# A mixture-of-experts block on one core: each expert's down part queued behind the next expert's gate and up part

## The chip, the core and the metric

The kernel runs on one core of one Trainium2 chip. The metric is the device time in microseconds of one execution; the time of a kernel is the median of its runs. The engines are named as in the profile: PE is TensorE (matmul), PEld its weight load, DVE is VectorE, ACT is ScalarE, POOL is GpSimd, SP is SyncE, from whose queue the loads are issued.

## The reference

One block over 256 tokens of width 1024: a mixer (sparse attention, a state-space branch and memory attention, gated and merged), a layer norm, a mixture of 32 experts with 4 experts for each token, and a last layer norm. The change touches the experts and the last norm:

```python
h = _layer_norm(DEEPNORM_ALPHA * h + mix, ln1_g[l], ln1_b[l])
...
logits = (xt @ w_router + b_router).astype(F32)
top_val, top_idx = lax.top_k(logits, TOP_K)          # TOP_K = 4 of 32
gate = jax.nn.softmax(top_val, axis=-1)
...
def expert_block(args):
    xb, e = args
    gu = xb @ w_gate_up[e] + b_gate_up[e]            # 1024 x 2048
    g, lin = jnp.split(gu, 2, axis=-1)
    g = jnp.minimum(g, SWIGLU_LIMIT)
    lin = jnp.clip(lin, -SWIGLU_LIMIT, SWIGLU_LIMIT)
    act = g * jax.nn.sigmoid(SWIGLU_ALPHA * g) * (lin + 1.0)
    return act @ w_down[e] + b_down[e]               # 1024 x 1024
...
out = jnp.zeros((T + 1, D), ys.dtype).at[slot_tok].add(ys)[:T]   # weighted by gate
...
h = _layer_norm(DEEPNORM_ALPHA * h + ffn, ln2_g[l], ln2_b[l])
```

All of it is float32. The weights of the experts alone are 32 x 12 MiB.

## The kernel before, in words

The program is written with tiles; a scheduler orders the instructions of each engine by a simulated run of the program and draws an instruction ahead of an earlier one where it is ready sooner. Each engine then works through its own list in order.

**The front** (lines 175 to 980) is the mixer, the first norm and the router. It keeps its data in slots of 8 KB a partition: tags u, w, s and z with 11, 3, 4 and 4 slots (L47). The weights of the experts go into the same slots. `chunk` (L73) loads one chunk of 1 MiB from SP's queue (L76). `load_chunk(e, c)` (L155) loads chunk c of expert e: chunks 0 to 7 are rows of `w_gate_up`, 8 to 11 of `w_down`; the tag comes from PATTERN (L48) by a running index over all chunks, so the slots are used in turn. `load_some` (L169) loads the first five chunks while the front still works.

**The experts** (L1006 to L1116). `expert` is called 32 times in a Python loop. Each call handles up to 64 tokens of its expert (CAP). Its parts, in program order:

- Gather (L1009 to L1029): `oh` marks the token of each of the 64 places. 48 bf16 matmuls (three bf16 parts of the activations, two token tiles, eight feature tiles) pick the tokens into two PSUM tiles, `xg0` and `xg1`, of four feature tiles each. DVE multiplies each half by the norm's gain, POOL adds the norm's offset: `xT`.
- `pw` (L1034): two transposes of the gate weights, read by DVE into `ohT` and `gs`. `pw` and `pt` are two buffers of the tag "pt".
- Gate and up (L1042 to L1054): bias matmuls, then for each of 8 chunks four matmul pairs into PSUM `pg` and `pl`; the two column halves go to partitions 0 to 63 and 64 to 127. A chunk's slot is free when both `pg` and `pl` matmuls have read it.
- `last()` (L1055), the combination of the expert before: eight matmuls (L1098) scatter its scaled result `ys` to the tokens, DVE adds them to `acc` (L1100).
- SwiGLU in two halves of 256 columns on DVE and ACT (L1064 to L1073), with four transposes into `pt`, copied by ACT into `aT`.
- Down (L1077 to L1084): two PSUM tiles `py`, in the banks of the tags "pg" and "pl"; a bias matmul each, then 32 matmuls over 4 chunks.
- Eviction (L1088 to L1090): ACT scales `py` by `gs`, DVE forms the remainder: `ys`, one buffer for each half.

At expert 0 `then` adds the residual, at expert 1 it counts whether an expert has more than 64 tokens; the loop for such experts (L1130 to L1157) has no turns with these inputs. At expert 31 the last norm's vectors are spread (L1109 to L1112).

**The last norm** (L1119 to L1178). `statistics` over four quarters, the mean and variance, then on three quarters ACT subtracts the mean and POOL multiplies by the gain, on the fourth DVE does both (L1168 to L1176), while DVE forms the inverse root (`inv_sqrt`, L103: 12 instructions on two values each). Then DVE scales and adds on each quarter (L1177) and the quarter is stored, token tile 0 from SP's queue, token tile 1 from ACT's (L1178).

Of the kernel before, what the change touches and what calls it, by code (L numbers as in the profile page):

```python
# [23 lines left out]
NT = 2  # L24
KT = 8
# [33 lines left out]
def block_kernel(ctx: ExitStack, tc: tile.TileContext, a: dict, out: bass.AP):  # L59
# [19 lines left out]
    def tt(o, x, y, op):  # L79
        V.tensor_tensor(o, x, y, op=op)  # L80
# [925 lines left out]
    def expert(mp, pm, gu, dn, pick_e, pos_e, gate_e, slots, then=None, last=None):  # L1006


        sel = mp.tile([128, CAP], BF, tag="sel", name="sel")  # L1009
# [8 lines left out]
        for i in range(2):  # L1018
            ks = slice(4 * i, 4 * i + 4)
            xg = pm.tile([128, 4, CAP], F32, tag=f"xg{i}", name="xg", bufs=1)  # L1020
            for k in range(4):
                n = 0
                for b in range(3):
                    for t in range(NT):
                        PE.matmul(xg[:, k, :], hb[t][b][:, (4 * i + k) * 128:(4 * i + k + 1) * 128], oh[:, t, :],  # L1025
                                  start=n == 0, stop=n == 5)
                        n += 1
            tt(xT[:, ks], xg, lc[:, 0, ks, None].to_broadcast([128, 4, CAP]), OP.mult)
            gg(xT[:, ks], xT[:, ks], lc[:, 1, ks, None].to_broadcast([128, 4, CAP]), OP.add)  # L1029
# [7 lines left out]
        ohT = mp.tile([128, 256], F32R, tag="ohT", name="ohT")  # L1037
        gs = mp.tile([128, 1], F32, tag="gs", name="gs")
# [6 lines left out]
        def up(p_, o, lhsT, w, start, stop):  # L1045
            for hf in range(2):
                PE.matmul(p_[hf * 64:(hf + 1) * 64, :], lhsT, w[:, o + hf * 512:o + (hf + 1) * 512],  # L1047
                          start=start, stop=stop)
# [11 lines left out]
        pt = pm.tile([128, 512], F32, tag="pt", name="pt", bufs=2)  # L1060
        aT = mp.tile([128, 512], F32, tag="aT", name="aT", bufs=1)
        halves = [slice(i * 256, (i + 1) * 256) for i in range(2)]
        g2 = gc.rearrange("p (q c i) -> p q c i", q=2, i=2)
        for sl in halves:  # L1064
            V.tensor_scalar(gc[:, sl], pg[:, sl], LIMIT, None, op0=OP.min)  # L1065
            S.activation(sg[:, sl], gc[:, sl], AF.Sigmoid, scale=SWIGLU_ALPHA)  # L1066
            tt(gc[:, sl], gc[:, sl], sg[:, sl], OP.mult)
        for i, sl in enumerate(halves):
            V.tensor_scalar(lin[:, sl], pl[:, sl], LIMIT, -LIMIT, op0=OP.min, op1=OP.max)
            V.scalar_tensor_tensor(gc[:, sl], lin[:, sl], 1.0, gc[:, sl], op0=OP.add, op1=OP.mult)  # L1070
            for c in (2 * i, 2 * i + 1):
                PE.transpose(pt[:, c * 128:(c + 1) * 128], g2[:, i, :, c % 2], ident)  # L1072
            S.activation(aT[:, sl], pt[:, sl], AF.Copy)  # L1073
        a4 = aT.rearrange("p (c h s) -> p h c s", c=4, h=2)


        pys = [pm.tile([128, 512], F32, tag=tag, name="py", bufs=1) for tag in ("pg", "pl")]  # L1077
        for hf, py in enumerate(pys):
            PE.matmul(py[0:64, :], sel, bias[:, 2 * DFF + hf * 512:2 * DFF + (hf + 1) * 512], start=True, stop=False)  # L1079
        for k in range(0, KT, 2):  # L1080
            for hf, py in enumerate(pys):
                for j in range(2):
                    PE.matmul(py[j * 64:(j + 1) * 64, :], a4[:, k // 4, k % 4 + j, :], dn(k + j, hf),  # L1083
                              start=k + j == 1, stop=k == 6)  # L1084
        ys = []
        for hf, py in enumerate(pys):

            y2 = mp.tile([128, 2, 512], F32R, tag=f"ys{hf}", name="ys", bufs=1)  # L1088
            S.activation(y2[:, 0], py, AF.Copy, scale=gs)  # L1089
            V.scalar_tensor_tensor(y2[:, 1], py, gs, y2[:, 0].bitcast(F32), op0=OP.mult, op1=OP.subtract)  # L1090
            ys.append(y2)

        def combine():
            for hf in range(2):
                for t in range(NT):
                    pc = pm.tile([128, 512], F32, tag="pc", name="pc", bufs=2)
                    for i in range(2):
                        PE.matmul(pc, ohT[:, t * 128:(t + 1) * 128], ys[hf][:, i], start=i == 0, stop=i == 1)  # L1098
                    o = acc[:, t, hf * 512:(hf + 1) * 512]
                    tt(o, o, pc, OP.add)  # L1100
        return combine

    gb2 = vectors(a["ln2_g"], a["ln2_b"])
    last = None
# [166 lines left out]
```

## Time and profile before

| What | Value |
|---|---|
| Median of 3 runs | 1286.26 us (1285.35 to 1784.17) |
| The profiled execution's own time | 1288.12 us |
| Its span, first to last instruction | 1286.4 us |
| Mean granted TensorE clock | 0.983 |
| PE busy | 1216.3 us, 95% of the span |
| PEld busy | 607.8 us, 47% |
| DVE busy | 585.9 us, 46% |
| ACT busy | 294.0 us, 23% |
| POOL busy | 72.6 us, 6% |
| DMA | 451.98 MB, mean 351 GB/s |

Times in the views count from the first instruction of the span. The matmuls' ends are modelled, so a busy PE is not PE at its peak. A wait is put down to what came last before it ended. A chunk is one DMA issue of 1024 KB. The experts' matmuls begin at 348 us and end at 1270 us.

### The profile page before, as it was taken

The page shows a single profiled execution, that of the slowest core. Times are in us where ns is not written, and L with a number is a line of the kernel's source. Part 1 is how long each engine was busy: PE and PEld are TensorE (multiplying, and loading weights), DVE is VectorE, ACT ScalarE, POOL GpSimd, SP SyncE. Part 2 cuts the span into 40 slices and gives each one's busy share as a digit, 9 for nine tenths or more (in the row PEclk, how much of TensorE's full clock was granted, in tenths as well). Part 3 has the DMA queues.
Part 4 walks back from the last instruction along what each step waited for, and adds up shares of the span by engine and source line. Part 5 has one row for each costly group of instructions (what it writes and reads, how often), then busy time and mean ns, then how long its engine had stood idle before and what let it go on. Part 6 is the DMA issues. An engine that isn't in the chain of part 4 may idle for free. (4 is left out here: it accounts for less than half of the span.)

```text
span 1286.4 us, 18050 instructions
## 1 busy us (share of the span) xinstructions
PE 1216.3 (95%) x7277; PEld 607.8 (47%) x7278; DVE 585.9 (46%) x1326; ACT 294.0 (23%) x580; POOL 72.6 (6%) x139
## 2 busy tenths in 40 slices
PE   7999999999799999999999999999999999999994
PEld 6657888788544443333333333333334333333331
DVE  6599986657832432333334333333334333333225
ACT  4245569963210110100001101000011011000011
POOL 1000000000200000000000000000001000000001
PEclk9999999999799999999999999999999999999997
DMA  7335535447799999999999999999999999999991
GB/s 271 108 129 192 195 133 153 158 167 314 265 406 422 426 426 427 426 426 426 427 426 426 427 425 427 426 426 426 427 425 427 426 426 426 426 427 426 426 415 66
DMA packets 65335, 451.98 MB, mean 351 GB/s; under 512 B 8896, under 2 KB 9056, under 8 KB 11360
## 3 DMA queue, kind: packets, MB, share of 16 engines
q1 hardware_dynamic: 64960, 450.26, 85.1%
q8 instruction: 59, 0.97, 0.3%
q10 hardware_dynamic: 288, 0.52, 0.1%
q14 instruction: 28, 0.23, 0.0%
HBM read 449.70 MB, written 1.05 MB: 350 GB/s over the span
## 5 line engine op out<-in xcount | busy, mean ns | idle before, releaser
L1047 PE MATMUL pg<-w,xT 128*64 128x512 f32 x1024 | 266.0, 597 | 0.0
L1047 PE MATMUL pl<-w,xT 128*64 128x512 f32 x1024 | 262.7, 592 | 0.0
L1083 PE MATMUL py<-w,aT 128*64 128x512 f32 x1024 | 230.2, 602 | 0.0
L1065 DVE TENSOR_SCALAR gc<-pg 128x256 f32<-128x256 f32 x64 | 24.2, 420 | 336.3 <-PE pg L1047 336.3
L1090 DVE SCALAR_TENSOR_TENSOR ys<-py,gs,ys 128x512 fp32r<-128x512 f32 x64 | 48.0, 751 | 210.9 <-ACT ys L1089 207.5
L1047 PEld LDWEIGHTS pl<-w,xT 128*64 128x64 f32 x1024 | 78.8, 137 | 133.6 <-issue 125.7
L1083 PEld LDWEIGHTS py<-w,aT 128*64 128x64 f32 x1024 | 71.3, 138 | 133.8 <-issue 127.8
L1047 PEld LDWEIGHTS pg<-w,xT 128*64 128x64 f32 x1024 | 71.9, 136 | 129.6 <-issue 116.0
L1066 ACT ACTIVATE sg<-gc 128x256 f32<-128x256 f32 x64 | 23.1, 408 | 477.0 <-DVE gc L1065 477.0
L80 DVE TENSOR_TENSOR h<-h,pc 128x512 f32<-128x512 f32 x128 | 82.6, 684 | 57.0 <-PE pc L1098 55.3
L83 POOL TENSOR_TENSOR xT<-xT,lc 128x256 f32<-128x256 f32 x64 | 44.9, 702 | 784.7 <-PE py L1079 778.4
L1089 ACT ACTIVATE ys<-py,gs 128x512 fp32r<-128x512 f32 x64 | 44.0, 687 | 195.1 <-PE py L1083 195.1
L1098 PE MATMUL pc<-ys,ohT 128*128 128x512 f32 x256 | 85.5, 435 | 0.9 <-DVE h L80 0.8
L1098 PEld LDWEIGHTS pc<-ys,ohT 128*128 128x128 f32 x256 | 40.2, 188 | 65.8 <-issue 35.1
L187 DVE TENSOR_TENSOR hl<-w,hl 128x1024 fp32r<-128x1024 f32 x48 | 58.2, 1222 | 18.1 <-ACT hl L186 17.8
L201 PE MATMUL mm<-hTh,hl 128*128 128x256 f32 x192 | 56.0, 292 | 0.1
L199 PE MATMUL mm<-hTh,hl 128*128 128x256 f32 x192 | 55.8, 291 | 0.0
L200 PE MATMUL mm<-hTl,hl 128*128 128x256 f32 x192 | 55.4, 289 | 0.0
L186 ACT ACTIVATE hl<-w 128x1024 fp32r<-128x1024 f32 x48 | 49.8, 1053 | 17.8 <-PE mm L201 9.6
L1073 ACT ACTIVATE aT<-pt 128x256 f32<-128x256 f32 x64 | 24.5, 383 | 120.8 <-PE pt L1072 117.4
L1025 PE MATMUL xg<-oh,hb 128*128 128x64 bf16 x1280 | 51.3, 195 | 0.9 <-DVE oh L1015 0.9
L1025 PEld LDWEIGHTS <-hb 128*128 128x128 bf16 x1280 | 47.5, 99 | 9.3 <-issue 8.2
(399 smaller groups left out, 1518.9 us busy)
## 6 DMA issues: line engine op xcount, KB each, us to landing
w<-in_w_gate_up SPq DMA_DIRECT2D x256, 1024.0 KB, 19.6
w<-in_w_down SPq DMA_DIRECT2D x128, 1024.0 KB, 19.6
w<-in_w_g SPq DMA_DIRECT2D x12, 1024.0 KB, 4.9
w<-in_w_s_glu SPq DMA_DIRECT2D x4, 1024.0 KB, 5.5
w<-in_w_o SPq DMA_DIRECT2D x4, 1024.0 KB, 5.8
w<-in_w_memk SPq DMA_DIRECT2D x2, 1024.0 KB, 10.5
w<-in_w_u SPq DMA_DIRECT2D x2, 1024.0 KB, 8.6
w<-in_w_memv SPq DMA_DIRECT2D x2, 1024.0 KB, 5.1
```

What stands on the lines that cost most here:

```text
L80: V.tensor_tensor(o, x, y, op=op)
L83: G.tensor_tensor(o, x, y, op=op)
L186: S.activation(hi, src, AF.Copy)
L187: (eng or V).tensor_tensor(lo, src, hi.bitcast(F32), op=OP.subtract)
L199: PE.matmul(o, lhsT(0), rhs(0), start=start, stop=False)
L200: PE.matmul(o, lhsT(0), rhs(1), start=False, stop=False)
L201: PE.matmul(o, lhsT(1), rhs(0), start=False, stop=stop)
L1025: PE.matmul(xg[:, k, :], hb[t][b][:, (4 * i + k) * 128:(4 * i + k + 1) * 128], oh[:, t, :], start=n == 0, stop=n == 5)
L1047: PE.matmul(p_[hf * 64:(hf + 1) * 64, :], lhsT, w[:, o + hf * 512:o + (hf + 1) * 512], start=start, stop=stop)
L1083: PE.matmul(py[j * 64:(j + 1) * 64, :], a4[:, k // 4, k % 4 + j, :], dn(k + j, hf), start=k + j == 1, stop=k == 6)
L1090: V.scalar_tensor_tensor(y2[:, 1], py, gs, y2[:, 0].bitcast(F32), op0=OP.mult, op1=OP.subtract)
L1098: PE.matmul(pc, ohT[:, t * 128:(t + 1) * 128], ys[hf][:, i], start=i == 0, stop=i == 1)
```

## The change

The load order: after the eight gate and up chunks of expert e come the four down chunks of expert e-1. `expert` no longer runs its down part; it returns two functions, `transposes` and `down`. The loop calls expert e, then the down part of expert e-1, then the transposes of expert e (`issue_after` puts what stands in its block behind the named instruction on that engine); the bias matmuls of gate and up follow the transposes of the expert before. The combination of expert e-2 stands in expert e's gate and up part, one half of the columns after chunk 3 and one after chunk 5. At the end the combination of expert 30, the down part of expert 31 and its combination follow. PSUM: `xg` is one tile of one bank, evacuated whole by one DVE and one POOL instruction; `pw` and `pt` share one buffer; `py0` and `py1` have banks of their own. `sel`, `ohT` and `gs` have three buffers. SwiGLU runs over 512 columns at a time. The last norm: DVE alone subtracts, multiplies and scales, after the inverse root, by token tiles; a token tile's first quarter is stored from SP's queue, the second from ACT's.

```diff
@@ load_some
+    order = [(0, c) for c in range(KT)]
+    for e in range(1, 4):
+        order += [(e, c) for c in range(KT)] + [(e - 1, c) for c in range(KT, 12)]
...
-            early.append(load_chunk(len(early) // 12, len(early) % 12))
+            early.append(load_chunk(*order[len(early)]))
@@ expert
-        for i in range(2):
-            ks = slice(4 * i, 4 * i + 4)
-            xg = pm.tile([128, 4, CAP], F32, tag=f"xg{i}", name="xg", bufs=1)
...
-            tt(xT[:, ks], xg, lc[:, 0, ks, None].to_broadcast([128, 4, CAP]), OP.mult)
-            gg(xT[:, ks], xT[:, ks], lc[:, 1, ks, None].to_broadcast([128, 4, CAP]), OP.add)
+        xg = pm.tile([128, KT, CAP], F32, tag="xg", name="xg", bufs=1)
...
+        tt(xT, xg, lc[:, 0, :, None].to_broadcast([128, KT, CAP]), OP.mult)
+        gg(xT, xT, lc[:, 1, :, None].to_broadcast([128, KT, CAP]), OP.add)
...
-        pw = pm.tile([128, 512], F32, tag="pt", name="pw", bufs=2)
+        pw = pm.tile([128, 512], F32, tag="pt", name="pw", bufs=1)
...
-        up(pg, 0, sel, bias, True, False)
-        up(pl, DFF, sel, bias, True, False)
+        with tc.issue_after(after.ins) if after else ExitStack():
+            up(pg, 0, sel, bias, True, False)
+            up(pl, DFF, sel, bias, True, False)
         for k in range(KT):
             w = gu(k)
             up(pg, 0, xT[:, k, :], w, False, k == KT - 1)
-            up(pl, DFF, xT[:, k, :], w, False, k == KT - 1)
-        if last:
-            last()
+            end = up(pl, DFF, xT[:, k, :], w, False, k == KT - 1)
+            if last and k in (3, 5):
+                with tc.issue_after(end.ins):
+                    last(k // 5)
...
+        V.tensor_scalar(gc, pg, LIMIT, None, op0=OP.min)
+        S.activation(sg, gc, AF.Sigmoid, scale=SWIGLU_ALPHA)
+        V.tensor_scalar(lin, pl, LIMIT, -LIMIT, op0=OP.min, op1=OP.max)
+        tt(gc, gc, sg, OP.mult)
+        V.scalar_tensor_tensor(gc, lin, 1.0, gc, op0=OP.add, op1=OP.mult)
+        def transposes():
+            pt = pm.tile([128, 512], F32, tag="pt", name="pt", bufs=1)
+            aT = mp.tile([128, 512], F32, tag="aT", name="aT", bufs=1)
+            for c in range(4):
+                end = PE.transpose(pt[:, c * 128:(c + 1) * 128], g2[:, c // 2, :, c % 2], ident)
+            S.activation(aT, pt, AF.Copy)
+            ats.append(aT.rearrange("p (c h s) -> p h c s", c=4, h=2))
+            return end
+        def down():
+            a4 = ats[0]
+            pys = [pm.tile([128, 512], F32, tag=f"py{i}", name="py", bufs=1) for i in range(2)]
...
+            def combine(*hfs):
+                for hf in hfs:
...
+            return combine, end
+        return transposes, down
@@ the loop over experts
+        weights(e, 0, KT)
+        if e:
+            weights(e - 1, KT, 12)
         if e == NE - 1:
+            weights(e, KT, 12)
...
+        last = None
+        if before:
+            last, end = before[1]()
+            with tc.issue_after(end.ins):
+                after = part[0]()
+        else:
+            after = part[0]()
+        before = part
+    if last:
+        last(0, 1)
+    before[1]()[0](0, 1)
@@ the last norm
-    quarters = [(t, i, acc[:, t, i * 512:(i + 1) * 512]) for i in range(2) for t in range(NT)]
-    nmu = fin.tile([128, NT], F32)
-    V.tensor_scalar(nmu, mv[:, :, 0], -1.0, None, op0=OP.mult)
-    for t, i, o in quarters[:3]:
-        S.activation(o, o, AF.Identity, bias=nmu[:, t:t + 1])
-        gg(o, o, l2[:, 0, i], OP.mult)
+    quarters = [(t, i, acc[:, t, i * 512:(i + 1) * 512]) for t in range(NT) for i in range(2)]
...
     for t, i, o in quarters:
-        if (t, i) == (1, 1):
-            V.scalar_tensor_tensor(o, o, nmu[:, t:t + 1], l2[:, 0, i], op0=OP.add, op1=OP.mult)
+        V.scalar_tensor_tensor(o, o, mv[:, t, 0:1], l2[:, 0, i], op0=OP.subtract, op1=OP.mult)
         V.scalar_tensor_tensor(o, o, rs[:, t:t + 1], l2[:, 1, i], op0=OP.mult, op1=OP.add)
-        (S if t else nc.sync).dma_start(out[t * 128:(t + 1) * 128, i * 512:(i + 1) * 512], o)
+        (S if i else nc.sync).dma_start(out[t * 128:(t + 1) * 128, i * 512:(i + 1) * 512], o)
```

## Rows read from the trace of the kernel before

**Rows 1.** Busy time by stretches of the span (the columns: the stretch and its length in us, then busy us and instruction count of PE, PEld, DVE, ACT and POOL, the granted clock of TensorE as a share of full speed, the mean busy share of the DMA engines, and GB/s): the last stretch before the experts' steady stage, an early one, and one of the steady stage.

```profile
340.00:360.00 20.00, 17.16 (x136) 8.17 (x137) 14.04 (x45) 0.00 (x0) 3.25 (x6) 0.81 0.66 248
...
380.00:400.00 20.00, 19.50 (x132) 9.81 (x130) 7.41 (x20) 1.49 (x4) 1.59 (x3) 1.00 0.98 397
...
600.00:700.00 100.00, 96.47 (x554) 36.80 (x552) 33.82 (x72) 9.96 (x20) 5.21 (x9) 1.00 1.01 426
```

**Rows 2.** Whom the DMA queue of SyncE waited for after 500 us (waiter, what ended the wait: total us, times, longest us). L76 issues the weight loads.

```profile
SPq L76 <- DMA w<-in_w_gate_up: 410.5, 200, 3.4
SPq L76 <- DMA w<-in_w_down: 205.2, 99, 3.4
...
SPq L76 <- PE pl L1047: 8.7, 21, 2.9
SPq L76 <- PE py L1083: 6.6, 13, 1.9
```

**Rows 3.** Whom TensorE waited for between 500 and 1215 us, all rows of the answer (same columns).

```profile
PE py L1079 <- DVE lin L1069: 19.0, 24, 0.8
PE pt L1072 <- ACT aT L1073: 8.2, 25, 0.6
PE pt L1072 <- DVE gc L1070: 2.0, 2, 1.3
```

**Rows 4.** Timeline of TensorE over one expert of the steady stage (start us, us taken, engine, line, operation, tiles, count; in brackets the idle time just before it). Lines of the pages: L1047 gate and up, L1079 bias of the down part, L1083 down part, L1098 combination.

```profile
1019.86 1.03 PE L1047 MATMUL pl<-w,xT 128*64 128x512 f32 x4
...
1022.08 0.40 PE L1079 MATMUL py<-bias,sel 128*64 128x512 bf16 x1 [0.79 <-DVE lin L1069]
...
1025.29 7.09 PE L1083 MATMUL py<-w,aT 128*64 128x512 f32 x32
1032.37 0.73 PE L1098 MATMUL pc<-ys,ohT 128*128 128x512 f32 x2
...
1033.49 0.74 PE L1098 MATMUL pc<-ys,ohT 128*128 128x512 f32 x2
...
1036.24 1.20 PE L1098 MATMUL pc<-ys,ohT 128*128 128x512 f32 x4
...
1054.02 7.09 PE L1083 MATMUL py<-w,aT 128*64 128x512 f32 x32
```

**Rows 5.** Timeline of SyncE's queue: the issues of the last expert's weights (start us, us from the first to the end of the last issue, count).

```profile
1212.78 17.60 SPq L76 DMA_DIRECT2D w<-in_w_gate_up  x8
1232.48 7.65 SPq L76 DMA_DIRECT2D w<-in_w_down  x4
```

**Rows 6.** DMA issues by line, whole span: the loads of w_down (count, KB each, median us from issue to landing).

```profile
w<-in_w_down SPq DMA_DIRECT2D x128, 1024.0 KB, 19.6
```

**Rows 7.** Busy time by stretches of 1 us at the end of the transfers (columns as in group 1).

```profile
1258.00:1259.00 1.00, 0.82 (x4) 0.51 (x6) 0.00 (x0) 0.40 (x2) 0.00 (x0) 0.90 0.29 123
1259.00:1260.00 1.00, 1.00 (x4) 0.24 (x2) 0.00 (x0) 0.10 (x1) 0.00 (x0) 0.50 0.08 33
1260.00:1261.00 1.00, 1.00 (x4) 0.24 (x2) 0.00 (x0) 0.00 (x0) 0.00 (x0) 0.50 0.00 0
1261.00:1262.00 1.00, 1.00 (x6) 0.32 (x4) 0.00 (x0) 0.00 (x0) 0.00 (x0) 0.50 0.00 0
```

**Rows 8.** Timeline of all engines over the last expert and the final norm (columns as in group 4).

```profile
1239.83 1.08 PE L1047 MATMUL pg<-w,xT 128*64 128x512 f32 x4
...
1254.25 1.03 PE L1047 MATMUL pl<-w,xT 128*64 128x512 f32 x4
...
1258.61 8.78 PE L1083 MATMUL py<-w,aT 128*64 128x512 f32 x32
...
1266.64 0.69 ACT L1089 ACTIVATE ys<-py,gs 128x512 fp32r<-128x512 f32 x1 [7.54 <-PE py L1083]
...
1274.33 0.17 DVE L1167 TENSOR_SCALAR nmu<-mv 128x2 f32<-128x2 f32 x1
...
1275.33 3.70 POOL L83 TENSOR_TENSOR h<-h,l 128x512 f32<-128x512 f32 x3 [78.78 <-ACT h L1169]
1275.40 1.22 DVE L109 TENSOR_SCALAR nr_y<-nr_w 128x2 int32<-128x2 int32 x1
...
1279.09 0.16 DVE L117 SCALAR_TENSOR_TENSOR nr_y<-nr_w,nr_y 128x2 f32<-128x2 f32 x1
```

**Rows 9.** Groups of instructions between 600 and 1200 us, shapes kept apart: the two that evacuate the gather (busy us, mean ns of one, then idle time before and its releaser).

```profile
L83 POOL TENSOR_TENSOR xT<-xT,lc 128x256 f32<-128x256 f32 x42 | 29.5, 702 | 566.9 <-PE py L1079 566.9
...
L80 DVE TENSOR_TENSOR xT<-xg,lc 128x256 f32<-128x256 f32 x42 | 15.7, 416 | 0.0
```

**Rows 10.** Timeline of TensorE over the first two experts: first gate matmul, first part of expert 0's down part, first gate and first up-bias matmul of expert 1.

```profile
348.18 1.08 PE L1047 MATMUL pg<-w,xT 128*64 128x512 f32 x4
...
366.41 1.94 PE L1083 MATMUL py<-w,aT 128*64 128x512 f32 x8
...
376.29 5.74 PE L1047 MATMUL pg<-w,xT 128*64 128x512 f32 x25
381.45 0.38 PE L1047 MATMUL pl<-bias,sel 128*64 128x512 bf16 x1
```

**Rows 11.** Busy time by stretches of 5 us, just before the first expert's matmuls (columns as in group 1).

```profile
345.00:350.00 5.00, 5.00 (x78) 3.75 (x77) 3.57 (x14) 0.00 (x0) 1.22 (x2) 0.76 0.02 7
```

**Rows 12.** Timeline of all engines at the very end: the last products of the norm.

```profile
1280.55 2.74 DVE L1177 SCALAR_TENSOR_TENSOR h<-h,nr_y,l 128x512 f32<-128x512 f32 x4
```

More of the change, by code (lines that the diff above doesn't have):

```diff
@@ L1004, in block_kernel, with expert @@
     pm = main.enter_context(tc.tile_pool(name="pm", bufs=1, space=PSUM))
-    def expert(mp, pm, gu, dn, pick_e, pos_e, gate_e, slots, then=None, last=None):
-        sel = mp.tile([128, CAP], BF, tag="sel", name="sel")
+    def expert(mp, pm, gu, dn, pick_e, pos_e, gate_e, slots, then=None, last=None, after=None):
+        sel = mp.tile([128, CAP], BF, tag="sel", name="sel", bufs=3)
         G.tensor_copy(sel, pick_e.to_broadcast([128, CAP]))
@@ L1068, in expert @@
[L1068 to L1077, printed above, removed]
@@ L1093, in combine @@
[L1093 to L1101, printed above, removed]
-    gb2 = vectors(a["ln2_g"], a["ln2_b"])
-    last = None
+        V.tensor_scalar(gc, pg, LIMIT, None, op0=OP.min)
@@ new lines, in down @@
+        def down():
+            a4 = ats[0]
+            pys = [pm.tile([128, 512], F32, tag=f"py{i}", name="py", bufs=1) for i in range(2)]
+            for hf, py in enumerate(pys):
+                PE.matmul(py[0:64, :], sel, bias[:, 2 * DFF + hf * 512:2 * DFF + (hf + 1) * 512],
+                          start=True, stop=False)
+            for k in range(0, KT, 2):
+                for hf, py in enumerate(pys):
+                    for j in range(2):
+                        end = PE.matmul(py[j * 64:(j + 1) * 64, :], a4[:, k // 4, k % 4 + j, :], dn(k + j, hf),
+                                        start=k + j == 1, stop=k == 6)
+            ys = []
+            for hf, py in enumerate(pys):
+                y2 = mp.tile([128, 2, 512], F32R, tag=f"ys{hf}", name="ys", bufs=1)
+                S.activation(y2[:, 0], py, AF.Copy, scale=gs)
+                V.scalar_tensor_tensor(y2[:, 1], py, gs, y2[:, 0].bitcast(F32), op0=OP.mult, op1=OP.subtract)
+                ys.append(y2)
+            def combine(*hfs):
+                for hf in hfs:
+                    for t in range(NT):
+                        pc = pm.tile([128, 512], F32, tag="pc", name="pc", bufs=2)
+                        for i in range(2):
+                            PE.matmul(pc, ohT[:, t * 128:(t + 1) * 128], ys[hf][:, i], start=i == 0, stop=i == 1)
+                        o = acc[:, t, hf * 512:(hf + 1) * 512]
+                        tt(o, o, pc, OP.add)
+            return combine, end
@@ L1105, in block_kernel, with weights @@
+        return transposes, down
+    gb2 = vectors(a["ln2_g"], a["ln2_b"])
+    last = before = after = None
+    ws = {}
+    def weights(e, lo, hi):
+        for c in range(lo, hi):
+            ws[e, c] = chunks.pop(0) if chunks else load_chunk(e, c)
+    chunks = list(early)
     for e in range(NE):
-        cs = [early[c + 12 * e] if c + 12 * e < len(early) else load_chunk(e, c) for c in range(12)]
-        gw, dw = cs[:KT], cs[KT:]
+        weights(e, 0, KT)
+        if e:
+            weights(e - 1, KT, 12)
@@ L1112, in block_kernel @@
                     [128, 512], F32, tag="pc", name="pc", bufs=2)), AF.Copy)
-        last = expert(mp, pm, lambda k: gw[k], lambda k, c: dw[k // 2][:, k % 2 * 1024 + c * 512:k % 2 * 1024 + (c + 1) * 512],
-               stack[:, e:e + 1], lambda t: posm[:, t, e:e + 1], lambda t: gmat[:, t, e:e + 1], slot,
-               residual if e == 0 else further_blocks if e == 1 else None, last)
-    last()
+        part = expert(mp, pm, lambda k, e=e: ws[e, k],
+                      lambda k, c, e=e: ws[e, KT + k // 2][:, k % 2 * 1024 + c * 512:k % 2 * 1024 + (c + 1) * 512],
+                      stack[:, e:e + 1], lambda t: posm[:, t, e:e + 1], lambda t: gmat[:, t, e:e + 1], slot,
+                      residual if e == 0 else further_blocks if e == 1 else None, last, after)
+        last = None
[9 more added lines that the diff above has]
+    before[1]()[0](0, 1)
     main.close()
@@ L1154, in dn @@
                     return dws[k // 2][:, k % 2 * 1024 + c * 512:k % 2 * 1024 + (c + 1) * 512]
-                expert(op, opm, gu, dn, pick_e, lambda t: pos_e[:, t:t + 1], lambda t: gate_e[:, t:t + 1], slot)()
+                part = expert(op, opm, gu, dn, pick_e, lambda t: pos_e[:, t:t + 1], lambda t: gate_e[:, t:t + 1],
+                              slot)
+                part[0]()
+                part[1]()[0](0, 1)
         statistics()
```

41 lines of the change are left out of this document (12 added, 29 removed).

## The prediction

> **What bounds the kernel now.** First the stretches [rows 1]: which stage owns the time. In the stage of the experts the transfers run at a share of 1.01 and 426 GB/s while TensorE is 96% busy, so two engines look full at once. An expert is 12 chunks of 1 MiB, 12.58 MB: 29.5 us at that rate, 2.46 us a chunk. Second, what the DMA queue waits for [rows 2]: after 500 us it waits 615.7 us for earlier weight loads and 15.3 us for the two PE lines that give slots back. Slots are not short there; transfers pace transfers. Third, TensorE's own waits [rows 3]: 29.2 us over 25 experts, 1.17 us an expert, all on DVE or ACT around the SwiGLU, none on a transfer. TensorE never runs out of weights; it is behind them. One expert's timeline gives the pace [rows 4]: one down part starts at 1025.29 and the next at 1054.02, a period of 28.73 us, 0.77 us under the transfers' 29.5. So TensorE pays off, at 0.77 us an expert, a backlog that it had from the start.
>
> How much is left at the end? The last expert's gate and up chunks are issued in 17.60 us from 1212.78, its last down chunk at about 1239.8 [rows 5], and a chunk lands 19.6 us after its issue [rows 6]: the first of them at 1232.4, the very last at 1259.4. The windows agree: 33 GB/s between 1259 and 1260, then nothing [rows 7]. I take 1260.0 for the last landing and its signal. TensorE starts that expert at 1239.83, 7.4 us behind its first chunk, ends gate and up at 1255.28, starts down at 1258.61 and ends it at 1267.39 [rows 8]. The transfers would allow an end near 1262. After 1267.39 comes one serial chain (eviction, combination, statistics, norm, store), 20.7 us to the execution's 1288.12 us. So the transfers are the floor, and the change can win only what lies behind their end, and what they lose before 400 us.
>
> **The change part by part.**
>
> *The down part one expert later, with the load order.* Between gate and up (end 1020.89) and down (1025.29) TensorE now spends 4.40 us on the next gather, on transposes and on waits [rows 4]. With the previous expert's down part there, 7.08 us long, the SwiGLU has cover, and the 1.17 us of waits go: 28.73 - 1.17 = 27.56 us. No DMA is added or dropped: 12 issues an expert on SyncE's queue, slots dealt by the same running index, and the new order of loading is the new order of use, so no slot is held longer in the queue. Hence the transfers keep their 29.5 us and nothing of the 1.17 us an expert shows directly: it pays off the backlog. 7.4 us over 30 experts needs 0.25 us, so any period up to 28.48 us makes TensorE wait for transfers at the end. What is late next is the last chunk. Backwards from 1260.0: expert 30's last down chunk now lands four chunks earlier, 1250.2; its matmuls take a quarter of 7.09 us, 1.77 us: 1252.0. Next on TensorE stand four transposes, beside the eviction of expert 30 (0.69 us on ACT [rows 8] and, as an estimate, as much on DVE: about 1.5 us), then the combination of expert 30, eight matmuls, 0.73 + 0.74 + 1.20 = 2.67 us [rows 4]: 1256.2. The down part of expert 31 takes 7.09 us, its last chunk being there when its turn comes at 1261.5: end 1263.3. Gain 1267.4 - 1263.3 = 4.1 us. Bounds: 5.6 us (1261.8, if nothing stands before the last chunk) and 0 (the backlog stays).
>
> *PSUM regrouped: the gather.* It is now evacuated whole. A half costs 0.42 us on DVE and 0.70 us on GpSimd [rows 9], so the whole 2.24 us before the first gate matmul may start. In the steady stage it costs nothing as long as the gather is drawn a whole down part ahead, as it is today (before 1025.29, used after 1032.37); without that cover it costs up to 2.24 us an expert, about 1 us of it beside bias matmuls and transposes. For expert 0 there is no cover: the first gate matmul, at 348.18 [rows 10], needed one half and now needs both, 1.12 us more (bounds 0 and 2.24). The transfers stand still just then, 7 GB/s from 345 to 350 [rows 11], until that expert gives slots back, so this passes to all that follows: -1.1 us.
>
> *PSUM regrouped: own banks for the down part.* Today expert 1's gate part runs 25 matmuls from 376.29 before the first one of its up part, at 381.45, whose bank the down part still holds [rows 10]. A chunk is free only when both have read it, and from 380 to 400 the transfers make 397 instead of 427 GB/s [rows 1]: 20 x 30/427 = 1.4 us lost. With banks of their own that returns: +1.4 us (bounds 0 and 1.4).
>
> *One bank for both transposes.* The next expert's transposes wait for ACT's copy of the last ones, at most 0.8 us an expert as an estimate (two waits of up to 0.6 stand there today [rows 3]). Behind them queue the bias and gate matmuls. 27.56 + 0.8 = 28.36 is still under 28.48: cost 0, on the edge.
>
> *Combination in halves after chunks 3 and 5; SwiGLU at full width; three buffers for small tiles.* The same eight matmuls and four DVE adds an expert, on results that are then most of an expert old; SwiGLU has 7.08 us of cover except in expert 0, where eight chunks' slots are already free. 0, from -0.5 to +0.5.
>
> *Final norm.* Today the tiny DVE instructions of the inverse root run beside GpSimd's products (1275.33 to 1279.03): one takes 1.22 us there and 0.16 us after it [rows 8]. The scale is ready at 1280.55, and four wide instructions of 0.685 us end at 1283.29 [rows 12]. Without GpSimd the twelve tiny ones take some 0.21 us each (seven lie between 1279.09 and 1280.55): 1274.4 + 2.5 = 1276.9. Eight wide ones follow, 5.5 us: 1282.4. Gain 0.9 us (0.4 with 0.75 us for a wide one, 1.3 with 0.18 us for a tiny one). The last store follows as today.
>
> Sum: 4.1 - 1.1 + 1.4 + 0.9 = 5.3 us. 1288.12 - 5.3 = 1282.8 us on the profiled execution, which is 1.86 us above the median of the runs: 1281.0 us.
>
> **The clock.** At the end of the kernel before, TensorE does only crumbs between 1255.28 and 1258.61, and then the granted clock is 0.50 (1.2 GHz) from 1259 to 1262 [rows 7, 8]. Waits of 0.79 us, one in each expert [rows 4], left it at 1.00 [rows 1]. [...]
>
> **Rivals.**
>
> *The waits cost the clock.* At the half clock a chunk takes 3.54 us, more than its 2.46 us of transfer: the last down part takes 14.2 us from 1256.2 to 1270.4, 3.0 us later than today. 1288.12 + 3.0 - 1.2 - 1.86 = 1288.1 us. For it: the fall at 1259. Against it: no wait that the new order makes is as long as the 3.3 us before that fall. Chance 0.12.
>
> *The backlog stays.* The gather half exposed (1 us) with the wait for the shared bank (0.8) stops the period falling below 28.5. TensorE ends about as now, and the norm and a part of the hidden SwiGLU are won: 1.5 us, 1284.8 us. For it: the gather now stands behind the previous down part in program order. Against it: the scheduler draws it ahead today. Chance 0.15.
>
> *Slower: the gather alone on TensorE's path.* If in each expert nothing but bias and transposes stands between gather and gate, the 2.24 us, the bank wait of 0.8 and the evictions' hops are paid every time: 27.56 + 2.24 + 0.8 - 1 = 29.6 us. It decides from 28.83 on, where 30 x 0.10 us eats the 3 us won elsewhere; at 29.6 TensorE is the bound: 30 x 0.87 - 3 = 23 us more, 1309 us. Chance 0.06, a third of it above 2% (a period over 29.7).
>
> *More than forecast.* No step before 400 us loses and the last chunk finds TensorE free: 5.6 + 1.4 + 1.3 = 8.3 us, 1278, or less with a better start: 1275 to 1278. Chance 0.05.
>
> **How the numbers follow.** The forecast has 0.62; its own range is 1277 to 1285. To keep no more than 2 in 10 out, the range takes in the backlog case, the clock case and most of the better one: 1275 to 1288.5. A measurement of this kernel tells about 2% (25.7 us) from no change. Faster by that would need the matmuls to end before the weights are there: 0.01. Slower by that is a third of the slower rival and a little for a start that I misread: 0.03. The rest, 0.96, is within 2%.
>
> **What would show it right or wrong.** Right: DMA rows appear among TensorE's waits after 900 us; the last down part ends 1 to 4 us after the last packet; the window 380 to 400 shows 426 GB/s; the first gate matmul comes 1 us later; no tiny DVE instruction of the norm is over 0.3 us. Wrong: a period between gate parts over 28.5 us with waits on GpSimd before each; a clock under 1.00 in windows of the middle; transfers below 426 GB/s after 400 us, which would mean that the new order starves for slots.

## The result and the profile after

The changed kernel takes 1280.55 us (median of 12 runs, 1278.55 to 1284.24); the kernel before, on the same chip, 1287.44 us. The ratio is 0.9949, with a 95% interval of 0.9935 to 0.9964: 6.9 us less by the medians, inside the 2% that were called no change. The profiled execution took 1282.35 us (span 1280.7), against 1288.12: 5.77 us less, where 5.3 were forecast.

Lines have moved: gate and up stand at L1049, the bias of the down part at L1089, the down part at L1094, the combination at L1109, the gather at L1028, the transposes of the activations at L1079, the products of the last norm at L1205 and L1206.

First the stretches, the columns as in [rows 1, 7]:

```profile
345.00:350.00 5.00, 4.36 (x70) 2.86 (x67) 3.06 (x17) 0.00 (x0) 0.63 (x3) 0.73 0.38 152
...
380.00:400.00 20.00, 20.00 (x96) 6.89 (x93) 4.81 (x8) 2.60 (x4) 0.00 (x0) 1.00 1.01 428
600.00:700.00 100.00, 100.00 (x624) 44.44 (x622) 36.75 (x64) 10.31 (x16) 6.36 (x8) 1.00 1.01 426
...
1259.00:1260.00 1.00, 1.00 (x6) 0.29 (x4) 0.00 (x0) 0.00 (x0) 0.00 (x0) 1.00 0.41 172
1260.00:1261.00 1.00, 1.00 (x8) 0.39 (x6) 0.00 (x0) 0.00 (x0) 0.00 (x0) 1.00 0.04 16
```

From 380 to 400 the transfers make 428 GB/s, where they made 397; from 600 to 700 TensorE is 100% busy and not 96. The transfers end at nearly the same place: 172 GB/s in the last full microsecond, 16 in the next. The first row is not to be read against [rows 11] alone (152 GB/s, where it was 7): this execution began the experts later, as shown below, and its standstill lies in the next stretch, 36 GB/s from 350 to 355 us.

SyncE's queue from 500 to 1290 us (answers to [rows 2]: us in total, times, longest):

```profile
SPq L76 <- DMA w<-in_w_gate_up: 410.7, 200, 2.9
SPq L76 <- DMA w<-in_w_down: 207.1, 100, 2.9
```

It waits for earlier loads, 617.8 us in all, as before. What TensorE waits for, from 500 to 1215 us (answers to [rows 3]):

```profile
PE py L1094 <- DMA w<-in_w_down: 16.9, 32, 1.1
PE pg L1049 <- DMA w<-in_w_gate_up: 8.4, 17, 0.8
```

The 29.2 us of waits on DVE and ACT are gone. In their place stand 25.3 us on transfers, in 49 waits, the longest 1.1 us: TensorE has caught up, and now runs out of weights. The timeline of TensorE shows one late period, and the same 24 matmuls of two down parts of the early stage (answers to [rows 4]):

```profile
1006.64 1.94 PE L1094 MATMUL py<-w,aT 128*64 128x512 f32 x8 [0.55 <-DMA w<-in_w_down]
1008.51 0.32 PE L1028 MATMUL xg<-oh,hb 128*128 128x64 bf16 x5
...
1036.23 1.94 PE L1094 MATMUL py<-w,aT 128*64 128x512 f32 x8 [0.50 <-DMA w<-in_w_down]
```

```profile
555.60 5.37 PE L1094 MATMUL py<-w,aT 128*64 128x512 f32 x24
...
582.56 5.37 PE L1094 MATMUL py<-w,aT 128*64 128x512 f32 x24
```

From 555.60 to 582.56 a period is 26.96 us, one of nine alike from 507 to 750 us, in which TensorE waits for no transfer; from 1006.64 to 1036.23 it is 29.59, the pace of the transfers. (Between 384 and 440 us single periods are shorter and longer, 26.65 and 29.20, since one of them holds two gathers.) The gather of the next expert (1008.51) is drawn into the down part, a whole part ahead of its use. The start of the experts on TensorE (answers to [rows 10]):

```profile
343.44 0.18 PE L957 MATMUL mm<-selb,before 128*128 128x32 bf16 x1 [3.61 <-DVE selb L953]
...
345.62 1.06 PE L1089 MATMUL py<-bias,sel 128*64 128x512 bf16 x2
346.62 0.48 PE L1038 MATMUL pw<-ident,og 128*128 128x128 f32 x1
...
348.61 0.19 PE L1028 MATMUL xg<-oh,bias 128*128 128x64 bf16 x1
...
349.58 0.31 PE L1028 MATMUL xg<-oh,hb 128*128 128x64 bf16 x5 [0.64 <-DVE xT L80]
...
351.07 1.08 PE L1049 MATMUL pg<-w,xT 128*64 128x512 f32 x4
```

The row at 348.61 is the last matmul of expert 0's gather. In the kernel before, that matmul is:

```profile
348.06 0.19 PE L1025 MATMUL xg<-oh,bias 128*128 128x64 bf16 x1
```

And the end, last expert and norm (answers to [rows 8, 9]; 1252.83 is the last expert's transposes, 1257.84 the last 24 matmuls of its down part):

```profile
1250.96 1.94 PE L1094 MATMUL py<-w,aT 128*64 128x512 f32 x8 [0.47 <-DMA w<-in_w_down]
...
1252.83 0.74 PE L1079 MATMUL pt<-ident,gc 128*128 128x128 f32 x4
...
1257.84 5.37 PE L1094 MATMUL py<-w,aT 128*64 128x512 f32 x24
...
1269.76 0.28 DVE L1199 BATCH_NORM_AGGREGATE mv<-bs 128x2 f32<-128x12 f32 x2 [0.26 <-DVEq L1163]
1270.00 1.41 DVE L1205 SCALAR_TENSOR_TENSOR h<-h,mv,l 128x512 f32<-128x512 f32 x2
...
1271.40 1.41 DVE L1205 SCALAR_TENSOR_TENSOR h<-h,mv,l 128x512 f32<-128x512 f32 x2
...
1272.92 0.17 DVE L109 TENSOR_SCALAR nr_y<-nr_w 128x2 int32<-128x2 int32 x1
...
1274.88 2.74 DVE L1206 SCALAR_TENSOR_TENSOR h<-h,nr_y,l 128x512 f32<-128x512 f32 x4
```

The last down part ends at 1263.21, and not at 1267.39. From the aggregated statistics (1269.76) to the end of the last product (1277.62) it is 7.86 us, and was 9.27.

So on the profiled executions: by the packets of the trace, the last weight packet ends at 1260.45 us (1260.24 in the kernel before), 0.21 us later; the down part ends 2.76 us behind it and not 7.15, 4.39 us won; the norm gives 1.41; the rest differs by 0.18. -0.21 + 4.39 + 1.41 + 0.18 = 5.77 us. The distance behind the last packet repeats: it is 2.8 to 2.9 us in the traces of e1, e4, e6, e8 and e9 below, which keep the delayed down part, and 7.7 in e2, which doesn't have it.

The profiled execution also began the experts late. The router's last choice mask (`selb`) is written from 343.21 us (343.44 is its first use), and was from 341.71 before, though the instructions of TensorE and DVE up to there have the same order in both. Over the profiled executions of all kernels here this point lies between 338.8 and 344.6 us, and it passes on to the end: from it to the last weight packet it is 917.2 to 918.7 us in every kernel but e3, e4 and e5. The transfers run far below 426 GB/s there until expert 0 gives slots back. Of the 1.50 us 1.29 are gone by the last packet; but from mask to last packet two kernels with the same start differ by 0.9 us (917.24 here, 918.17 in e1). From 400 to 1230 us every kernel whose transfers are the floor moves 426.3 to 426.4 GB/s; what differs is mostly how many bytes are there by 400 us. This fits the spread of runs of one kernel, some 2 us to each side, and is a reason not to read a difference of 1 us from two profiles.

### The profile page after: what moved, and what is told of

Same layout as the page of the kernel before. It is cut to its first block, busy times and chain, and to the rows that moved or that the text cites. A ratio compares the mean times of both kernels' runs of the same rounds, so it can differ in the third digit from the quotient of the medians.

```text
span 1280.7 us, 17715 instructions
## 1 busy us (share of the span) xinstructions
PE 1218.5 (95%) x7277; PEld 613.7 (48%) x7278; DVE 582.4 (45%) x1168; ACT 283.5 (22%) x513; POOL 63.4 (5%) x104
## 5 line engine op out<-in xcount | busy, mean ns | idle before, releaser
L1049 PE MATMUL pg<-w,xT 128*64 128x512 f32 x1024 | 293.4, 606 | 8.6 <-DMA w<-in_w_gate_up 8.4
L1049 PE MATMUL pl<-w,xT 128*64 128x512 f32 x1024 | 284.6, 592 | 0.0
L1094 PE MATMUL py<-w,aT 128*64 128x512 f32 x1024 | 240.1, 599 | 18.1 <-DMA w<-in_w_down 17.9
L1049 PEld LDWEIGHTS pl<-w,xT 128*64 128x64 f32 x1024 | 94.6, 137 | 127.3 <-issue 104.6
L1094 PEld LDWEIGHTS py<-w,aT 128*64 128x64 f32 x1024 | 68.7, 136 | 160.0 <-issue 97.6
L1069 ACT ACTIVATE sg<-gc 128x512 f32<-128x512 f32 x32 | 20.2, 630 | 557.4 <-DVE gc L1068 557.4
L1049 PEld LDWEIGHTS pg<-w,xT 128*64 128x64 f32 x1024 | 73.9, 135 | 123.7 <-DMA w<-in_w_gate_up 60.5
L1109 PE MATMUL pc<-ys,ohT 128*128 128x512 f32 x256 | 77.0, 421 | 0.9 <-DVE h L80 0.8
L1109 PEld LDWEIGHTS pc<-ys,ohT 128*128 128x128 f32 x256 | 43.0, 188 | 57.8 <-issue 50.7
L83 POOL TENSOR_TENSOR xT<-xT,lc 128x512 f32<-128x512 f32 x32 | 41.6, 1300 | 456.1 <-DVE xT L80 456.1
L1028 PEld LDWEIGHTS <-hb 128*128 128x128 bf16 x1280 | 47.1, 98 | 29.8 <-issue 28.0
L1068 DVE TENSOR_SCALAR gc<-pg 128x512 f32<-128x512 f32 x32 | 22.1, 691 | 69.0 <-PE pg L1049 69.0
L1028 PE MATMUL xg<-oh,hb 128*128 128x64 bf16 x1280 | 51.6, 194 | 1.5 <-DVE oh L1020 0.9
L1041 DVE TENSOR_SCALAR ohT<-pw 128x256 fp32r<-128x256 f32 x32 | 13.5, 423 | 72.0 <-PE pw L1038 72.0
```

The lines of the kernel that those rows point to most:

```text
L1028: PE.matmul(xg[:, k, :], hb[t][b][:, k * 128:(k + 1) * 128], oh[:, t, :], start=n == 0, stop=n == 5)
L1049: m = PE.matmul(p_[hf * 64:(hf + 1) * 64, :], lhsT, w[:, o + hf * 512:o + (hf + 1) * 512], start=start, stop=stop)
L1094: end = PE.matmul(py[j * 64:(j + 1) * 64, :], a4[:, k // 4, k % 4 + j, :], dn(k + j, hf), start=k + j == 1, stop=k == 6)
```

## Experiments

All were timed in 5 rounds beside the kernel before, whose median was 1286.31 us with e1, e2, e3 and e6, 1286.4 with e4, e5, e7 and e8, and 1287.53 with e9.

**Are the transfers the floor now, and were they not before? (e4_less_after, e5_less_before)** Two experts' down parts load nothing and use chunks that are already there: 8 chunks of 1 MiB less. In the changed kernel:

```diff
+SKIP = (16, 20)
...
-        if e:
+        if e and e - 1 not in SKIP:
             weights(e - 1, KT, 12)
...
-                      lambda k, c, e=e: ws[e, KT + k // 2][:, k % 2 * 1024 + c * 512:k % 2 * 1024 + (c + 1) * 512],
+                      lambda k, c, e=e: ws[(e + 1, 4 + k // 2) if e in SKIP else (e, KT + k // 2)][:, k % 2 * 1024 + c * 512:k % 2 * 1024 + (c + 1) * 512],
```

> The changed kernel without the loads of experts 16's and 20's down weights (8 chunks of 384; those two down parts use chunks 4 to 7 of the next expert's gate and up weights instead, the matmuls stay the same). Theory (transfers are the floor, TensorE has about 2.9 us an expert to spare): all 8 x 2.46 = 19.7 us are won, 18 to 20 us faster than the changed kernel. Rival (TensorE's own chain is the bound all along, and its waits for loads are only the place where slack shows): under 8 us.

> The kernel before without the loads of experts 16's and 20's down weights (8 chunks of 384; those two down parts use chunks 4 to 7 of their own expert's gate and up weights). Theory (TensorE's backlog is the bound there: it never waits for a load): within 1.5 us of the kernel before, though the transfers end some 19 us earlier. Rival (the transfers are the bound in both): 15 to 20 us faster.

Measured: 1260.5 us (ratio 0.9800, 0.9786 to 0.9814), 20.0 us under the changed kernel (19.2 by the two ratios); and 1285.5 us (0.9989, 0.9977 to 1.0002), 0.9 under the kernel before. Eight chunks at 2.46 us are 19.7 us: the changed kernel gives all of it within the noise, the one before next to nothing. There the stretches at the end show why (e5, columns as above):

```profile
1240.00:1245.00 5.00, 5.00 (x22) 1.52 (x20) 2.13 (x4) 0.00 (x0) 0.00 (x0) 1.00 0.01 3
```

The last weight packet ended at 1237.3, and TensorE's last down part ends at 1264.9: TensorE was the bound, and a shorter transfer had nothing to give. This is the main point of the case, shown from both sides.

**What does the delay itself do? (e3_no_delay)** The changed kernel with each down part right behind its own transposes, the loads in the old order, and everything else as changed:

```diff
-        weights(e, 0, KT)
-        if e:
-            weights(e - 1, KT, 12)
+        weights(e, 0, 12)
...
-        if before:
-            last, end = before[1]()
-            with tc.issue_after(end.ins):
-                after = part[0]()
-        else:
-            after = part[0]()
-        before = part
...
+        part[0]()
+        last, after = part[1]()
```

> The changed kernel with each down part right behind its own transposes, and the loads in the old order; PSUM, SwiGLU at full width, combination in halves and the norm stay as changed. Theory (the period decides, and only the delayed down part covers the SwiGLU): the period between down parts rises from 26.64 us by the uncovered SwiGLU and the copy of the transposes, 1.9 to 2.7 us, to 28.5 to 29.3 us; TensorE never waits for a load after 500 us and ends behind the last packet by 7 us or more: 4 to 15 us slower than the changed kernel. Rival (own banks for the down part and the combination inside the gate part make the period, the delay adds nothing): period under 28 us, TensorE waits for loads after 1000 us, within 1.5 us of the changed kernel.

Measured: 1333.45 us, ratio 1.0371 (1.0341 to 1.0400): 47 us over the kernel before, 53 over the changed one. The sign was right and the size far off. TensorE's waits from 500 to 1215 us, and the first of SyncE's from 500 to 1290:

```profile
PE xg L1028 <- DVE xT L80: 33.3, 24, 1.4
PE py L1094 <- ACT aT L1080: 17.2, 23, 0.7
PE pt L1079 <- DVE gc L1072: 12.0, 24, 0.6
PE py L1089 <- DVE ys L1101: 7.2, 21, 0.3
```

```profile
SPq L76 <- PE pl L1049: 313.3, 182, 3.5
```

The first row is what I had left out: the next gather has one bank and waits for DVE to evacuate the last one, and that evacuation now queues behind the SwiGLU at full width. With the waits for the transposes, the copy and the bank it makes 69.7 us in 25 experts, 2.8 each; the period is 30.2 us (1003.94 to 1034.14), TensorE is the bound, and SyncE's queue waits for slots. So one gather bank and the SwiGLU at full width, which cost nothing under the delayed down part, cost much without it. No run has the delay with the gather and the SwiGLU in halves, so what the delay is worth by itself stays open.

**The norm alone (e1_old_norm, e2_new_norm)** The changed kernel with the old norm, and the kernel before with the new one: the last hunk of the diff undone, or alone. In e1:

```diff
+    for t, i, o in quarters[:3]:
+        S.activation(o, o, AF.Identity, bias=nmu[:, t:t + 1])
+        gg(o, o, l2[:, 0, i], OP.mult)
...
-        V.scalar_tensor_tensor(o, o, mv[:, t, 0:1], l2[:, 0, i], op0=OP.subtract, op1=OP.mult)
```

> The changed kernel with the last norm of the kernel before (products on ACT and GpSimd beside the inverse root). Theory: the norm is a serial part behind everything, so its whole 1.4 us comes back (7.86 us from the aggregation to the last product now, 9.27 us before): 1.4 us slower than the changed kernel, and tiny DVE instructions of about 1.2 us appear beside GpSimd's products. Rival: the norm's order of work is hidden by the stores, which end 3.1 us after the last product anyway: within 0.5 us.

> The kernel before with the last norm of the changed kernel and nothing else. Theory: 1.4 us faster than the kernel before, the last down part ending as before 7.4 us behind the last packet. Rival (hidden by the stores): within 0.5 us of the kernel before.

Measured: 1282.04 us (0.9966, 0.9954 to 0.9977), where the changed kernel has 0.9949; and 1285.24 us (0.9989, 0.9978 to 1.0001). That is 1.5 us against the changed kernel (2.2 by the two ratios) and 1.1 against the kernel before: some 1 to 2 us, at the edge of what the runs can tell. The traces tell it plainly: 9.27 us from aggregate to last product in e1, 7.86 in e2. DVE in e1:

```profile
1269.10 1.22 DVE L109 TENSOR_SCALAR nr_y<-nr_w 128x2 int32<-128x2 int32 x1
```

One tiny instruction, 1.22 us beside GpSimd's products; the same form is 0.17 us at 1272.92 in the changed kernel.

**The banks of the down part (e8_shared_banks)** The changed kernel with `py` in the banks of `pg` and `pl`, as before:

```diff
-pys = [pm.tile([128, 512], F32, tag=f"py{i}", name="py", bufs=1) for i in range(2)]
+pys = [pm.tile([128, 512], F32, tag=tag, name="py", bufs=1) for tag in ("pg", "pl")]
```

> The changed kernel with the down part's two PSUM tiles in the banks of gate and up again, as in the kernel before. Theory (own banks are what lets the down part follow gate and up at once): the down part waits for the SwiGLU's reads of both banks (1 to 1.6 us), the next gate part for the eviction (about 1.5 us): period 29 to 30 us instead of 26.64, TensorE behind the transfers to the end, 10 us slower than the changed kernel or more. Rival (the waits fall beside gather and transposes): period under 28.2 us, within 1.5 us.

Measured: 1279.97 us (0.9952, 0.9938 to 0.9967): the same as the changed kernel. My theory fell. TensorE's waits from 500 to 1215 us, and one early period:

```profile
PE py L1089 <- DVE lin L1070: 11.6, 24, 0.5
```

```profile
556.35 2.08 PE L1094 MATMUL py<-w,aT 128*64 128x512 f32 x8
...
584.22 2.08 PE L1094 MATMUL py<-w,aT 128*64 128x512 f32 x8
```

It costs 0.48 us of waiting an expert and a period of 27.87 us instead of 26.96, but that is still under the transfers' 29.5. The stretch from 380 to 400 us, here and then in e3:

```profile
380.00:400.00 20.00, 20.00 (x121) 9.04 (x118) 4.18 (x6) 2.60 (x4) 0.24 (x1) 1.00 1.01 428
```

```profile
380.00:400.00 20.00, 17.96 (x126) 7.47 (x122) 7.34 (x13) 0.63 (x1) 1.28 (x2) 1.00 1.01 426
```

With the new order and shared banks it is 428 GB/s, with own banks and the old order 426. So neither is needed where the other is there; which of them lifted the 397 GB/s, or something that both kernels share, the runs don't separate.

**The start (e6_start, e9_start2)** The rows of the start above show the bias of the down part (345.62) and a transpose (346.62) ahead of the gather at the half clock, 1.06 and 0.48 us, and the gather of expert 1 (349.58) ahead of the first gate matmul. In the kernel before that bias did not stand there. e6 evacuates the gather in halves and holds expert 1's gather behind expert 0's first gate chunk; e9 besides holds the bias and the transposes `pw` of expert 0 behind its gather. `hold` is the first gate chunk of expert 0 (given for expert 1), `gl` the last matmul of a gather:

```diff
+        with tc.issue_after(hold.ins) if hold else ExitStack():
             for k in range(KT):
...
-        tt(xT, xg, ...)
-        gg(xT, xT, ...)
+        for i in range(2):
+            ks = slice(4 * i, 4 * i + 4)
+            tt(xT[:, ks], xg[:, ks], ...)
+            gg(xT[:, ks], xT[:, ks], ...)
...
+            with tc.issue_after(gl.ins) if first else ExitStack():
                 for hf, py in enumerate(pys):
```

> The changed kernel with the gathered tokens evacuated in two halves (one bank still) and expert 1's gather issued behind expert 0's first gate chunk. Theory (the transfers are the floor and stand still until expert 0 gives its first slot back): the first gate matmul comes about 2.5 us earlier after the routing (1.4 us of gather, 1.1 us of evacuation), the last packet and the end move by the same: 1.5 to 2.5 us faster than the changed kernel. Rival (slots come free from the front just as fast, or the gain is lost at a later stall): the last packet stays, within 0.7 us.

> As e6_start (the gather evacuated in halves, expert 1's gather behind expert 0's first gate chunk), and for expert 0 the pw transposes and the bias matmuls of its down part are held behind its gather's last matmul. Theory: what stood between the router's last selb and the first gate matmul in e6_start was 1.06 us of py bias and 0.48 us of pw at half clock ahead of the gather; behind it they fill the 1.07 us wait for POOL's xT, so the distance falls from 7.39 to 6.0 to 6.4 us, and as TensorE is behind from there to some 750 us, the time comes 1 to 1.4 us under e6_start's: about 1279.8. Rival: expert 1's gather, drawn into expert 0's gate part, costs the same again (in e6_start the stretch from the first gate matmul to the end of the last down part was 913.58 us, 1.44 longer than in the changed kernel), and by the time TensorE has caught up transfers alone set the end: no difference from the changed kernel that 5 rounds show.

Measured: 1281.11 us (0.9964, 0.9951 to 0.9977) and 1282.4 us (0.9966, 0.9954 to 0.9977). Neither is faster than the changed kernel. TensorE in e6, then in e9, with e9's stretch from 345 to 350:

```profile
341.20 1.06 PE L1094 MATMUL py<-bias,sel 128*64 128x512 bf16 x2
342.19 0.48 PE L1041 MATMUL pw<-ident,og 128*128 128x128 f32 x1
...
346.18 1.08 PE L1052 MATMUL pg<-w,xT 128*64 128x512 f32 x4 [1.07 <-POOL xT L83]
```

```profile
347.18 0.40 PE L1029 MATMUL xg<-oh,hb 128*128 128x64 bf16 x4
...
350.17 0.62 PE L1096 MATMUL py<-bias,sel 128*64 128x512 bf16 x2
351.08 1.08 PE L1053 MATMUL pg<-w,xT 128*64 128x512 f32 x4 [0.29 <-POOL xT L83]
```

```profile
345.00:350.00 5.00, 4.10 (x56) 3.09 (x55) 3.37 (x22) 0.00 (x0) 0.68 (x3) 0.50 0.50 206
```

From the last choice mask to the first gate matmul it is 7.86 us in the changed kernel, 7.39 in e6 and 6.47 in e9. With the changed kernel's start it is 8.45 us in e1 and 7.59 in e8, so the 0.47 us of e6 are no more than executions differ by. In e6 bias and transpose still stand ahead (341.20, 342.19). In e9 they stand behind, and the whole gather runs in a stretch at a granted clock of 0.50; 6.0 to 6.4 was missed by a little. The changed kernel has 0.73 from 345 to 350 us, but that stretch begins 1.8 us after its mask and 0.4 us after e9's, so the two can't be set against each other, and that the new order held the clock down isn't shown. What is won there is given back: from the first gate matmul to the end of the last down part e9 takes 915.1 us, e6 913.6 and the changed kernel 912.1 (e1 912.6, e8 912.8). Why that stretch grows was not settled.

**The end (e7_last_halves)** e6, and the last expert's down weights loaded by column halves, so that its first output half is evicted and combined while the second one computes:

```diff
+    rows = a["w_down"][e, (2 * r + b) * 256:(2 * r + b + 1) * 256, hf * 512:(hf + 1) * 512]
+    nc.sync.dma_start(w[:, b * 1024:(b + 1) * 1024].rearrange("p (i d) -> p i d", i=2), ...)
```

> The kernel of the run with the earlier start, and the last expert's down weights loaded by column halves: its first output half is evicted, combined and summed while the second half's weights still land. Theory (behind the last packet stands a serial chain): the eviction, combination and statistics of one half leave the chain, about 2.3 us of the 6.6 us between the last down matmul and the aggregation: 2 to 2.5 us faster than the kernel with the earlier start, 3.5 to 5 us faster than the changed kernel. Rival (rows of 2 KB instead of 8 KB slow these last 4 MiB of loads by as much): no faster than the kernel with the earlier start.

Measured: 1280.94 us (0.9954, 0.9941 to 0.9967), no faster. The chain from the last matmul of the down part to the aggregation went from 6.56 us in e6 to 4.85, 1.71 us won as the theory had it, but TensorE came to that last matmul later. The last expert's transposes and the end of its down part, in e6 and then in e7:

```profile
1249.38 0.74 PE L1084 MATMUL pt<-ident,gc 128*128 128x128 f32 x4
...
1254.39 5.37 PE L1099 MATMUL py<-w,aT 128*64 128x512 f32 x24
```

```profile
1251.26 0.74 PE L1096 MATMUL pt<-ident,gc 128*128 128x128 f32 x4
...
1260.18 1.20 PE L1129 MATMUL pc<-ys,ohT 128*128 128x512 f32 x4
1261.31 1.94 PE L1111 MATMUL py<-w,aT 128*64 128x512 f32 x8
```

From the first row to the end of the last it is 10.38 us in e6 and 11.99 in e7, and in neither does TensorE wait for a transfer there. The combination of the first half (1260.18, 1.20 us) now stands ahead of the last eight matmuls. So 1.61 us of the 1.71 are lost on TensorE, which is the bound of these last microseconds; where the other 0.4 us go wasn't settled. The transfers are slower for a while, as the rival had it, 313 GB/s from 1246 to 1248 us; but the last packet ends 918.4 us after the mask, and 918.1 in e6. So the rival's time came, but the rows of 2 KB are not what took the gain.

## Why the prediction was right

*TensorE behind the weights.* Held, by e4 and e5. The backlog at the end was 7.15 us from last packet to last matmul (7.4 in the prediction), and is 2.76; 3.3 was forecast. With it falls the rival that the backlog stays: TensorE waits 25.3 us for transfers. But not all of the backlog was there "from the start". In the kernel before one late period, by the transposes from 1196.14 to 1229.50, is 33.36 us, 4.6 over the others. In it TensorE spreads the last norm's vectors, 4.35 us in three pieces, and one down part runs partly at the half clock, 8.56 us where 7.09 is usual [rows 4]:

```profile
1197.77 8.56 PE L1083 MATMUL py<-w,aT 128*64 128x512 f32 x32
```

```profile
1198.00:1200.00 2.00, 2.00 (x6) 0.54 (x6) 0.00 (x0) 0.26 (x1) 0.00 (x0) 0.50 1.01 422
```

So without that period the backlog at the end would have been some 2.5 us, as an estimate from 7.15 less 4.6; no run tested it.

*The down part delayed: 4.1 us.* Its end was forecast at 1263.3 and came at 1263.21, with the steps on the way at 1250.96 (1250.2 forecast, a wait for expert 30's last chunk) and 1252.83 (1252.0). The path is the one forecast; that the end agrees to 0.1 us is partly luck, since this execution was late (the chunk 0.8 us after its forecast) and TensorE's way from there took 12.25 us instead of 13.1. A part of the gain is the clock: the last down part took 8.78 us before, 1.69 over the 7.09, as the granted clock was 0.50 [rows 7, 8], and now it is 1.00 up to its end. The sum has this in its 7.09 without naming it. One detail differs: the first eight matmuls of the last down part are drawn ahead of the second half of the combination, and from 1252.83 on TensorE waits for no transfer. The period is 26.96 us and not 27.56: the waits of 1.17 us went as forecast, and 0.60 us more, which the rows don't split.

*The gather whole: -1.1 us.* The sign held, the working behind it did not. From the last choice mask the first gate matmul comes 1.4 us later, 7.86 us and not 6.47. The prediction took one half of the evacuation as exposed before and both now. But before, the gate part began at 348.18, as the gather's last matmul was ending (348.25): the first half was evacuated beside the second half of the gather, and nothing was exposed. Now 2.27 us lie between the end of the gather (348.80) and the gate, the 2.24 us of the whole. Of this 0.95 us came back, because the gather ends 5.59 us after the mask and not 6.54, in spite of the bias matmuls that now stand ahead of it. That the later gate costs the end 1.4 us isn't shown: e9, which wins it back there, was no faster.

*Own banks: +1.4 us.* The stretch came back as forecast, 428 GB/s; that the banks are its cause isn't shown, for e8 has it without them, and e3 has it with them and without the new order. The sum of this term and the last, +0.3 us, is not to be told from nothing in the traces: from mask to last packet it is 918.5 us in the kernel before and 917.7 in e2, 917.2 in the changed kernel, 918.2 in e1 and 917.5 in e8.

*One bank for both transposes, the combination in halves, SwiGLU, three buffers: 0.* No row on `pt`, `pw` or `pc` is left among TensorE's waits from 500 to 1215 us. e3 shows that this 0 stands on the cover of the down part.

*The norm: 0.9 us.* It gave 1.41. The eight wide instructions take the forecast 5.5 us (1.41 a pair for the first four, 2.74 for the last four), though four of them, which need only the mean, were drawn ahead of the inverse root. The mis-sized term is the tiny ones: 2.5 us were forecast, and between the end of the fourth wide one (1272.81) and the start of the fifth (1274.88) it is 2.07, as some run beside the wide ones. The wide ones also begin 0.24 us after the aggregation, where 0.38 was taken. The Trainium skill's page "SBUF — State Buffer", section "Terms", says that DVE and GpSimd share a port pair, which one of them holds for a whole instruction while the other stands still. The trace agrees: 1.22 us beside GpSimd's products, 0.17 without them.

*The rival on the clock.* It fell: 49 waits for transfers from 500 to 1215 us, none over 1.1 us, and the granted clock is 1.00 in every stretch of the rows from 380 to 1261 us, that from 1259 included, where it was 0.50 [rows 7]. No wait here lowered it, up to 1.1 us. The prediction's row for the other side was too kind, though: in the kernel before the clock also fell to 0.50 from 1198 to 1200 us, after TensorE had waited 0.79 and 1.34 us around one bias matmul. The Trainium skill's page "TensorE: Matmul & The Clock Gate", section "HAM oscillation — how this bites in real kernels", tells of a kernel that falls to the half clock at every wait for DMA; there each wait is longer than the matmuls ahead of it. Here the waits are at most 1.1 us and a chunk's eight matmuls take 1.94, so no run here shows that case.

*The slower rival.* It didn't come. e3 comes near its period, 30.2 us where 29.6 was worked out, but by other waits: none of its rows has the gate part waiting for the gather's evacuation. TensorE waits there for the gather's bank, the transposes and the copy. 30 periods of 1.47 us over the 28.73 [rows 4] make 44 of its 47 us.

## What to carry to other kernels

Where two engines both look full, ask which one waits for the other, and how far the one behind is when the other ends: that distance is all that a better order can win, and here it was 4.4 of 7.2 us. A quick proof is to leave out some bytes: the time follows them or it does not. A step that is free under another's cover should be priced without it too, because taking the cover away cost 53 us here.

## What the runs showed that was not expected

The transfers don't end at once. The changed kernel's stretches up to their end:

```profile
1252.00:1254.00 2.00, 2.00 (x13) 1.10 (x10) 1.02 (x2) 1.68 (x3) 0.00 (x0) 1.00 0.81 344
1254.00:1256.00 2.00, 2.00 (x12) 0.96 (x11) 1.67 (x3) 0.28 (x1) 0.00 (x0) 1.00 0.65 274
1256.00:1258.00 2.00, 2.00 (x9) 0.83 (x8) 0.52 (x1) 0.00 (x0) 0.00 (x0) 1.00 0.53 225
1258.00:1260.00 2.00, 2.00 (x10) 0.61 (x10) 0.77 (x2) 0.00 (x0) 0.00 (x0) 1.00 0.47 201
```

The DMA share, 1.00 from 1250 to 1252 us, falls to 0.81, 0.65, 0.53 and 0.47 over the last eight microseconds, at 344, 274, 225 and 201 GB/s: 1.32 MB less than at 426 GB/s, some 3.1 us. The rate falls in the same way in the kernel before. Which of the 16 engines end early, and why, the rows don't show; no run tried to even it out. From 1252.83 on TensorE waits for no transfer, so here it isn't this tail that sets the end.

Three tiny DVE instructions beside GpSimd's products cost some 3.1 us more than without them (some 1.2 against 0.17 us each), and the three wide products that were kept off DVE for it would have taken 2.1 us there (1.41 a pair). Sharing that work out lost.
